# One plain chunk and two opened pairs at the start of every feed-forward block

## The chip, the cores and the metric

The kernel runs on one core of a Trainium2 chip. The metric is the device time of one execution in microseconds; lower is better. Before the change it is 2757.24 us, the median of three runs (2756.95 to 2757.96).

## What is computed

A trunk of two layers over 768 tokens (512 of one batch, 256 of another) of width 1024. Each layer is a feed-forward block, a token mixer (a gated linear recurrence in the first layer, windowed attention in the second) and a second feed-forward block. So there are four feed-forward blocks, called f0, f1, f2 and f3 here in order of time. The one that matters:

```python
def swiglu_ffn(x, w1, w2):
    gate, up = jnp.split(x @ w1, 2, axis=-1)
    return (jax.nn.silu(gate) * up) @ w2
# in each layer, twice:
x = x + 0.5 * swiglu_ffn(rmsnorm(x, g), w1, w2)
```

`w1` is 1024 x 5632 (2816 gate and 2816 up columns), `w2` is 2816 x 1024, all in float32.

## The kernel before, in words

**Precision.** Each float32 operand is split into a high part, cast by ACT, and a low part, which VectorE gets by subtracting the high part again (`split`, lines 354 to 356; for weights lines 217 and 218). A product of two operands is three matmuls: high x high, high x low, low x high (`mm3`, lines 348 to 352; `product`, lines 544 to 557). Only the low part of the weight named p5 in the first projection is subtracted by GpSimd ("POOL" in the profile), on line 218.

**Chunks and pairs.** The 2816 hidden columns are 22 chunks of 128, and the tokens are two halves of 384. A chunk that is computed plainly (`up_plain`, line 526) takes 48 matmuls of 128x384 for each token half: 8 blocks of the width, gate and up, three matmuls each. All others are done as a "pair" (`up_pair`, line 559): gate and up against the two halves of the width and the two token halves are a 2x2 matrix product, done by seven products p1 to p7 of 12 matmuls each, 84 in place of 96. p1 needs the operand `b00` and p2 needs `b10` (the two halves of the width, token half 0); p3 needs `b11` (token half 1); p7, p5, p6 and p4 need the factors t3, t1, t2 and t4, each formed by subtractions from blocks of both token halves. The weights need sums too: "third" (`a21 += a22`) and the weight s3 of p7 are made by transfers that add on landing, issued by GpSimd (`into`, line 150); "second" (`a11 += a21`) and "fourth" (`a12 += a11`) are VectorE additions on line 224, pinned to their place in the program.

**The start of a feed-forward block.** At that point the normalised input of token half 1 isn't ready yet. So the first two chunks (PLAIN = 2) are done plainly: token half 0 of both, then half 1 of both. Meanwhile three deferred steps are run from a list at six fixed places among the matmuls of half 0 (`run_later`, line 534): two that transpose token half 1 into blocks (`turn`), and `sums` (line 475), which forms the factors in eight subtractions of 128x768 and splits each (`mix`, lines 456 to 473; in f0 a step for the normalisation comes ahead of them). It does so one half of the width's blocks after the other (kp = 0, then 1), and t1, t4, t3, t2 in each.

**Order and buffers.** Instructions are recorded in the order of the code; a scheduler then sets each engine's order from what they need, but for those pinned. Each engine runs its own list strictly in order. Weights are loaded by SP's queue into four raw buffers of 512 KB (`load_next`, line 153) and are split ahead of use into eight slots `w` (`stage_next`, `ahead`). PSUM has eight banks. In the profile `wr` is a raw weight, `s` the tile of s3, `w` a split weight, `big` an operand or a factor, `tA` a hidden result, `ps` a PSUM bank, `x` the residual.

Of the kernel before, what the change touches and what calls it, by code (L numbers as in the profile page):

```python
# [16 lines left out]
P = 128  # L17
D = 1024
DFF = 2816
NC = D // P  # L20
# [34 lines left out]
class Trunk:  # L55
# [97 lines left out]
    def load_next(self):  # L153
        key, srcs, shape, how = self.queue.pop(0)
        if how in (TOK, OUT):
            self.loaded.append((len(srcs), self.tok_steps(key, srcs, how), 4))
            return
        raws = []
        for src in srcs:
            t = self.wp.tile([P, 1024], F32, tag="wr", name=self.name("wr"), bufs=RAWBUFS)  # L160
            raw = t[:, : shape[0] * shape[1]].rearrange("p (a b) -> p a b", a=shape[0])
            if len(srcs) < 4:
# [7 lines left out]
        free = 4  # L170
        if self.more.get(key):
            tail = self.tail_steps(key, self.more[key], how)
            steps = [step for both in zip(steps, tail) for step in both]
            free = 8
        self.loaded.append((len(raws), steps, free))

    def wtile(self):
        return self.wp.tile([P, 1024], F32R, tag="w", name=self.name("w"), bufs=WBUFS)
# [8 lines left out]

        return [(2, go)]

    def quad_steps(self, key, raws, srcs, order):  # L190
        nc = self.nc
        flat = lambda t: t.rearrange("p a b -> p (a b)")
        up = len(raws) == 2
        if up:
            a11, a12, a21, a22 = (flat(t[:, h : h + 4, :]) for t in raws for h in (0, 4))
            three = [srcs[1].rearrange("(k p) c -> p k c", p=P)[:, :4, :]]
        else:
            a11, a12, a21, a22 = (flat(t) for t in raws)
            three = [srcs[2][:, i : i + 1, :] for i in range(2)]
        s3 = []  # L200
        for i, src in enumerate(three):
            t = self.wp.tile([P, 512], F32, tag="s3", name=self.name("s3"), bufs=2)
            self.last_load = nc.sync.dma_start(t.rearrange("p (a b) -> p a b", a=src.shape[1]), src)
            self.into(t, a11[:, i * 512 : (i + 1) * 512])
            s3.append(t)
        self.into(a21, a22)

        def split(name, srcs, eng=None):
            if up:
                w = self.wtile()  # L210
                hi, lo = w[:, :512], w[:, 512:]
            else:
                hi, lo = self.wtile(), self.wtile()
            n = srcs[0].shape[-1]
            for i, src in enumerate(srcs):
                h, l = (t[:, i * n : (i + 1) * n] for t in (hi, lo))
                nc.scalar.copy(h, src)  # L217
                (eng or nc.vector).tensor_sub(l, src, h.bitcast(F32))  # L218
# [5 lines left out]
        add = {"second": lambda: nc.vector.tensor_add(a11, a11, a21), "fourth": lambda: nc.vector.tensor_add(a12, a12, a11)}  # L224
# [83 lines left out]
    def stage_next(self):  # L308
        if not self.loaded:
            self.load_next()  # L310
        steps = self.loaded[0][1]
        n, go = steps.pop(0)
        go()
        self.held += n
        if not steps:
            self.loaded.pop(0)
        inuse = lambda e: e[0] if len(e[1]) > e[2] or e[0] < 4 else 0
# [15 lines left out]
    def ahead(self):  # L333
        while self.queue or self.loaded:
            if not self.loaded:
                self.load_next()
            if self.held + self.loaded[0][1][0][0] > WBUFS:
                return
            self.stage_next()

# [132 lines left out]
        put("t2", b11)  # L473

    def sums(self):
        for kp in range(2):
            tiles = (self.tn[(i // 2, i % 2)][:, kp] for i in range(4))
            self.mix(*tiles, lambda name, src: self.put(name, kp, src))

    def spill_factors(self):  # L480
        self.kept = {}
# [22 lines left out]
            self.later(self.sums)  # L504

    def plan_ffn(self, tag, w1, w2):
        def up(i):
            gate, up = (w1[:, c * P : (c + 1) * P] for c in (i, NF + i))
            if i < PLAIN:
                self.plan((tag, i, 0), gate, (NC, P))  # L510
                self.plan((tag, i, 1), up, (NC, P))
            else:
                self.plan_quad((tag, i), (gate, up), (NC, P), UP)
# [12 lines left out]
    def up_plain(self, tag, j, half):  # L526
        pss = []
        for c in range(2):
            wh, wl = self.take((tag, j, c))
            ps = self.ps(H)  # L530
            for k in range(NC):
                b = self.operand(f"b{k // 4}{half}", k % 4)
                self.mm3(ps, (wh[:, k, :], wl[:, k, :]), b, k == 0, k == NC - 1)
                if half == 0 and k in (((), (2, 6)), ((3, 7), (3, 7)))[j][c]:
                    self.run_later()
            if half:
                self.done((tag, j, c))
            pss.append(ps)
        t = self.tmp(H)
        self.nc.scalar.activation(t, pss[0], AF.Silu)  # L540
        self.nc.vector.tensor_mul(t, t, pss[1])
        return t
# [16 lines left out]
    def up_pair(self, tag, j, opened=None):  # L559
# [117 lines left out]
    def ffn(self, tag, next_row):  # L677
        for g in range(GROUPS):
# [952 lines left out]
```

## Time and profile before

| | |
|---|---|
| median of three runs | 2757.24 us |
| the profiled execution, its own time | 2759.27 us |
| its span | 2757.5 us |
| granted TensorE clock | 0.999 |
| TensorE (PE) busy | 2736.1 us, 99% |
| VectorE (DVE) busy | 2201.0 us, 80% |
| ACT busy | 1396.5 us, 51% |
| GpSimd (POOL) busy | 460.7 us, 17% |

Times in the profile are microseconds from the start of the span. A timeline row is: start, duration, engine, line, operation, output <- inputs, shape and count; in brackets stands the idle time of the engine just before it and what ended that. A group's row ends with its busy time and the mean of one in ns, then the idle time of the engine ahead of them. A row with "min/median/max" has those of one instruction in ns. A row of a transfer has KB each and the median us from issue to landing. A row of the waits has the total, the number of times and the longest.

### The profile page before, as it was taken

To read this page: it belongs to the slowest core of one execution; us is meant where nothing else is said; L and a number is where in the kernel's file an instruction comes from. 1 tells how busy PE (TensorE), PEld (TensorE's weight loads), DVE (VectorE), ACT (ScalarE), POOL (GpSimd) and SP (SyncE) were. 2 spreads that over 40 slices of the span, in tenths; PEclk is the share of its full clock that TensorE was granted. 3 is DMA by queue.
4 is the path that set the end of the run, shared out by engine and by line. 5 is a ranking of instruction groups with operands and counts; after the bars stand their busy time and mean duration, and the time that the engine had idled before them with its cause. 6 is when DMAs were issued, how large, how long until landed. Compare 5 with 4: busy or idle time off the path is not lost. (4 is left out here: it accounts for less than half of the span.)

```text
span 2757.5 us, 40950 instructions
## 1 busy us (share of the span) xinstructions
PE 2736.1 (99%) x15081; PEld 2547.1 (92%) x15081; DVE 2201.0 (80%) x3766; ACT 1396.5 (51%) x2621; POOL 460.7 (17%) x507
## 2 busy tenths in 40 slices
PE   8999999999999999999999999999999999999998
PEld 8999999989999889999998999999888889999997
DVE  8788788767887888788878887887847868788877
ACT  6344444634455675444455543444458855444453
POOL 2111121200000101211120121112005611211120
PEclk9999999999999999999999999999999999999999
DMA  6554556751122743555454355545424422655453
GB/s 171 132 122 116 126 140 167 217 153 39 39 60 65 201 121 82 145 134 127 114 138 126 77 145 128 126 118 142 130 77 112 89 69 73 146 134 128 116 135 111
DMA packets 355048, 330.46 MB, mean 120 GB/s; under 512 B 14664, under 2 KB 271648, under 8 KB 354848
## 3 DMA queue, kind: packets, MB, share of 16 engines
q1 hardware_dynamic: 303744, 225.61, 27.6%
q0 software_dynamic: 46800, 88.76, 18.3%
q10 hardware_dynamic: 4304, 13.49, 1.4%
q8 instruction: 118, 1.93, 0.3%
q14 instruction: 82, 0.67, 0.1%
HBM read 226.87 MB, written 15.73 MB: 88 GB/s over the span
## 5 line engine op out<-in xcount | busy, mean ns | idle before, releaser
L549 PE MATMUL ps<-big,w 128*128 128x384 f32 x6720 | 1168.5, 334 | 0.0
L549 PEld LDWEIGHTS ps<-big,w 128*128 128x128 f32 x6720 | 1165.7, 188 | 1.4
L217 ACT CAST w<-wr 128x512 fp32r<-128x512 f32 x600 | 417.2, 706 | 651.6 <-PE ps L549 300.1
L218 DVE TENSOR_TENSOR w<-wr,w 128x512 fp32r<-128x512 f32 (+1 forms) x520 | 436.1, 842 | 138.1 <-ACT w L217 122.3
L615 PE MATMUL ps<-w,big 128*128 128x512 f32 x2016 | 460.7, 389 | 0.0
L615 PEld LDWEIGHTS ps<-w,big 128*128 128x128 f32 x2016 | 377.9, 188 | 78.8 <-DVE x L675 0.6
L151 POOL DMA_DIRECT2D s<-wr x126 | 110.5, 884 | 1220.7 <-DMA s<-in_ffn_w_dram 324.7
L675 DVE SCALAR_TENSOR_TENSOR x<-ps,x 128x512 f32<-128x512 f32 x420 | 272.7, 684 | 13.7 <-PE ps L647 13.1
L350 PE MATMUL ps<-big,w 128*128 128x384 f32 x640 | 219.2, 344 | 1.5 <-ACT w L184 1.0
L351 PE MATMUL ps<-big,w 128*128 128x384 f32 x640 | 215.1, 336 | 0.4 <-DVE big L356 0.3
L352 PE MATMUL ps<-big,w 128*128 128x384 f32 x640 | 214.5, 335 | 0.0
L355 ACT CAST big<-tA 128x384 fp32r<-128x384 f32 x308 | 153.6, 513 | 101.6 <-DVE tA L583 34.2
L356 DVE TENSOR_TENSOR big<-tA,big 128x384 fp32r<-128x384 f32 x308 | 176.3, 585 | 5.3 <-ACT big L355 3.4
L151 POOL DMA_DIRECT2D wr<-wr x109 | 95.3, 874 | 510.2 <-DMA wr<-in_ffn_w_dram 175.1
L831 PE MATMUL ps<-w,big 128*128 128x512 f32 x756 | 177.1, 392 | 0.1
L647 PE MATMUL ps<-w,big 128*128 128x512 f32 x756 | 174.5, 391 | 0.7 <-DVE x L675 0.6
L647 PEld LDWEIGHTS ps<-w,big 128*128 128x128 f32 x756 | 141.3, 188 | 30.5 <-DVE x L675 1.5
L831 PEld LDWEIGHTS ps<-w,big 128*128 128x128 f32 x756 | 140.5, 188 | 29.2 <-DVE w L356 0.6
L218 POOL TENSOR_TENSOR w<-wr,w 128x512 fp32r<-128x512 f32 x80 | 130.4, 1630 | 169.7 <-ACT w L217 152.6
L224 DVE TENSOR_TENSOR wr<-wr,wr 128x512 f32<-128x512 f32 (+1 forms) x120 | 123.6, 1030 | 20.4 <-issue 20.2
L350 PEld LDWEIGHTS ps<-big,w 128*128 128x128 f32 x640 | 120.1, 188 | 2.5 <-ACT w L184 1.3
L351 PEld LDWEIGHTS ps<-big,w 128*128 128x128 f32 x640 | 120.4, 188 | 1.4 <-DVE big L356 1.2
(219 smaller groups left out, 3647.3 us busy)
## 6 DMA issues: line engine op xcount, KB each, us to landing
wr<-in_ffn_w_dram SPq DMA_DIRECT2D x256, 512.0 KB, 4.0
s<-wr POOLq DMA_DIRECT2D x126, 256.0 KB, 4.5
s<-in_ffn_w_dram SPq DMA_DIRECT2D x120, 256.0 KB, 3.2
wr<-wr POOLq DMA_DIRECT2D x80, 256.0 KB, 3.9
wr<-in_hg_w_in_dram SPq DMA_DIRECT2D x32, 512.0 KB, 3.9
wr<-wr POOLq DMA_DIRECT2D x29, 512.0 KB, 4.6
spill<-x ACTq DMA_DIRECT2D x12, 512.0 KB, 3.9
kept<-big POOLq DMA_DIRECT2D x8, 768.0 KB, 7.9
```

The costliest lines, as they stand in the source:

```text
L151: self.nc.gpsimd.dma_start(out, src, accum_op=ALU.add)
L217: nc.scalar.copy(h, src)
L218: (eng or nc.vector).tensor_sub(l, src, h.bitcast(F32))
L350: nc.tensor.matmul(out, a[0], b[0], start=first, stop=False)
L351: nc.tensor.matmul(out, a[0], b[1], start=False, stop=False)
L352: nc.tensor.matmul(out, a[1], b[0], start=False, stop=last)
L356: self.nc.vector.tensor_sub(lo, src, hi.bitcast(F32))
L549: self.nc.tensor.matmul(ps, a[x], b[y], start=first and k == 0 and i == 0, stop=k == 3 and i == 2, skip_group_check=True,)
L615: nc.tensor.matmul(ps, a[x], w[y], start=name == chain and kp == 0 and q == 0, stop=kp == 1 and q == 2, skip_group_check=True,)
L647: nc.tensor.matmul(ps, a[x], w[y], start=name == chain and k == 0 and q == 0, stop=k == 2 and q == 2, skip_group_check=True,)
L675: self.nc.vector.scalar_tensor_tensor(x, ps, c, x, ALU.mult, ALU.add)
L831: nc.tensor.matmul(ps, x[:, sl], y, start=fresh and k == 0 and q == 0, stop=k == 3 and q == 2, skip_group_check=True,)
```

## The change

PLAIN becomes 1: only the first chunk of a block is done plainly. The next two chunks are pairs that are opened early (OPENED = 2, new function `opened_pair`): the order on PE is plain half 0, p1 of both opened pairs, p2 of both, plain half 1, then the remaining five products of the first pair and of the second. The two opened pairs are loaded as one entry that fills the four raw buffers, and their "second" and "fourth" weight sums are made by transfers (`moved=True`) and no longer by VectorE. `sums` now goes factor by factor: t3 for both kp, then t1, t2, t4. The deferred steps are run at two places in the up columns of plain half 0, behind the two p1 and behind the two p2. The 19 pairs after that and the second projection stay; which of its raw buffers an entry holds is now said by a function of the steps left. Line numbers shift: the weight split is line 228 (218 before), the transfer 153 (151), the operand split 370 (356), the subtractions of `sums` 495 (458, 459, 469 and 470), the multiply behind the plain chunk 564 (541).

GpSimd's list at the start of f1, before: the transfers for the first pair behind the plain chunks (chunk 2) and the next, p5's split of the one (line 218), transfers for the second projection's weights, p5's split of the other.

```order
L151 DMA s_1300_9150<-wr_9146 128x512
L151 DMA wr_9148<-wr_9148 128x512
L151 DMA s_1325_9262<-wr_9258 128x512
L151 DMA wr_9260<-wr_9260 128x512
L218 TENSOR_TENSOR w_9523<-wr_9148,w_9523 128x512
L151 DMA s_1392_9732<-wr_9724 128x512
L151 DMA s_1393_9735<-wr_9724 128x512
L218 TENSOR_TENSOR w_9667<-wr_9260,w_9667 128x512
```

And after: the eight transfers for both opened pairs, then p5's split of the first and of the second opened pair (line 228), then the next pair's first transfer.

```order
L153 DMA s_1305_9165<-wr_9157 128x512
L153 DMA wr_9159<-wr_9159 128x512
L153 DMA s_1306_9169<-wr_9161 128x512
L153 DMA wr_9163<-wr_9163 128x512
L153 DMA wr_9157<-wr_9159 128x512
L153 DMA wr_9161<-wr_9163 128x512
L153 DMA wr_9157<-wr_9157 128x512
L153 DMA wr_9161<-wr_9161 128x512
L228 TENSOR_TENSOR w_9428<-wr_9159,w_9428 128x512
L228 TENSOR_TENSOR w_9559<-wr_9163,w_9559 128x512
```

p5's splits of two pairs now stand next to each other behind eight transfers; the two rows of the opened pairs' "second" sums (`wr_9157<-wr_9159` and `wr_9161<-wr_9163`) and the two of their "fourth" are new there.

VectorE's list at the same place in f1, before: the end of the sums, with two weight splits and a multiply of a plain chunk among them (line 541, one input `ps` in PSUM).

```order
L356 TENSOR_TENSOR big_9399<-big_9344,big_9399 128x2x384
L356 TENSOR_TENSOR big_9402<-big_9179,big_9402 128x2x384
L459 TENSOR_TENSOR big_9305<-big_9179,big_9305 128x768
L218 TENSOR_TENSOR w_9489<-wr_9146,w_9489 128x512
L469 TENSOR_TENSOR big_9179<-big_9179,big_9344 128x768
L356 TENSOR_TENSOR big_9407<-big_9305,big_9407 128x2x384
L470 TENSOR_TENSOR big_9227<-big_9227,big_9179 128x768
L218 TENSOR_TENSOR w_9492<-s_1300_9150,w_9492 128x512
L541 TENSOR_TENSOR tA_9527<-tA_9527,ps_9495 128x384
L356 TENSOR_TENSOR big_9412<-big_9227,big_9412 128x2x384
L356 TENSOR_TENSOR big_9415<-big_9344,big_9415 128x2x384
L356 TENSOR_TENSOR big_9418<-big_9179,big_9418 128x2x384
```

After: from t2's first split to the multiply of the plain chunk's half 1 (line 564), the next step with an input in PSUM.

```order
L370 TENSOR_TENSOR big_9444<-big_9324,big_9444 128x2x384
L370 TENSOR_TENSOR big_9448<-big_9198,big_9448 128x2x384
L370 TENSOR_TENSOR big_9452<-big_9198,big_9452 128x2x384
L495 TENSOR_TENSOR big_9246<-big_9246,big_9198 128x768 x2
L228 TENSOR_TENSOR w_9476<-wr_9157,w_9476 128x512
L370 TENSOR_TENSOR big_9456<-big_9246,big_9456 128x2x384
L370 TENSOR_TENSOR big_9460<-big_9246,big_9460 128x2x384
L228 TENSOR_TENSOR w_9492<-wr_9157,w_9492 128x512
L228 TENSOR_TENSOR w_9520<-wr_9159,w_9520 128x512
L228 TENSOR_TENSOR w_9531<-s_1306_9169,w_9531 128x512
L228 TENSOR_TENSOR w_9562<-wr_9161,w_9562 128x512
L564 TENSOR_TENSOR tA_9565<-tA_9565,ps_9534 128x384
```

The multiplies that stood among the sums are gone from there but for half 0's, which stands near the start of the sums (ten rows ahead of the piece shown); the additions of line 224 are gone, and five weight splits of the opened pairs stand between the last factor and the next step from PSUM.

The diff, cut to its core:

```diff
--- before.py
+++ after.py
-PLAIN = 2
+PLAIN = 1
+OPENED = 2
...
+OPEN = ("p1", "p2", "p7", "p5", "p3", "p6", "p4")
...
+        elif how == OPEN:
+            a, b = (self.quad_steps((key[0], i + PLAIN), raws[2 * i : 2 * i + 2], srcs[2 * i : 2 * i + 2], how, True) for i in range(OPENED))
+            steps = [a[0], b[0], a[1], b[1], *a[2:], *b[2:]]
...
+        if how == OPEN:
+            inuse = lambda left: 4 if left > 5 else 2
...
+        if moved:
+            add = {"second": lambda: self.into(a11, a21), "fourth": lambda: self.into(a12, a11)}
+            behind, pin = {"p1": "second", "p2": "fourth"}, lambda ins: None
...
     def sums(self):
-        for kp in range(2):
-            tiles = (self.tn[(i // 2, i % 2)][:, kp] for i in range(4))
-            self.mix(*tiles, lambda name, src: self.put(name, kp, src))
+        sub = self.nc.vector.tensor_sub
+        b = lambda kp: [self.tn[(i // 2, i % 2)][:, kp] for i in range(4)]
+        for name, out, x, y in (("t3", 3, 1, 3), ("t1", 1, 0, 1), ("t2", 0, 0, 3), ("t4", 2, 2, 0)):
+            for kp in range(2):
+                t = b(kp)
+                sub(t[out], t[x], t[y])
+                self.put(name, kp, t[out])
 
     def spill_factors(self):
...
+            elif i == PLAIN:
+                srcs = [w for j in range(OPENED) for w in halves(i + j)]
+                self.plan_quad((tag, "open"), srcs, (NC, P), OPEN)
...
-                if half == 0 and k in (((), (2, 6)), ((3, 7), (3, 7)))[j][c]:
+                if half == 0 and c and k in (2, 6):
                     self.run_later()
...
+    def opened_pair(self, tag, j):
+        nc = self.nc
+        key = (tag, j)
+        a, v = self.ps(H), self.tmp(H)
+        p = lambda name, ps, first, last: self.product(key, name, FACTOR[name], ps, first, last)
+        p("p1", a, True, False)
+        nc.scalar.copy(v, a)
+        self.ahead()
+        yield
+        p("p2", a, False, True)
+        nc.scalar.activation(a, a, AF.Silu)
+        self.ahead()
+        yield
+        b, c, d = (self.ps(H) for _ in range(3))
+        w, t = (self.tmp(H) for _ in range(2))
+        p("p7", c, True, False)
+        nc.scalar.copy(w, c)
+        self.ahead()
+        p("p5", d, True, False)
+        nc.vector.tensor_sub(w, w, d)
+        self.ahead()
+        p("p3", d, False, True)
+        self.ahead()
+        p("p6", b, True, True)
+        nc.vector.tensor_sub(v, v, b)
+        nc.vector.tensor_add(d, v, d)
+        nc.scalar.activation(d, d, AF.Silu)
+        nc.vector.tensor_sub(w, w, v)
+        nc.vector.tensor_mul(w, w, d)
+        yield 1, w
+        self.ahead()
+        p("p4", c, False, True)
+        nc.vector.tensor_sub(t, c, v)
+        nc.vector.tensor_mul(t, t, a)
+        yield 0, t
         self.ahead()
...
+            first = {}
             if g == 0:
-                ts = {}
-                for half in range(2):
-                    for j in range(PLAIN):
-                        t = ts[2 * j + half] = self.up_plain(tag, j, half)
-                        name = f"b{j}{half}"
-                        if name != "b01":
-                            put(name, t, 0)
-                gather(ts, 0)
+                ts = {0: self.up_plain(tag, 0, 0)}
+                put("b00", ts[0], 0)
+                first = {i + PLAIN: self.opened_pair(tag, i + PLAIN) for i in range(OPENED)}
+                for _ in range(2):
+                    for pair in first.values():
+                        next(pair)
+                    self.run_later()
+                ts[1] = self.up_plain(tag, 0, 1)
                 self.run_later(len(self.deferred))
             for kp in range(2):
-                if g == 0 and kp == 0:
-                    continue
-                ts = []
+                if g or kp:
+                    ts = {}
                 for j in range(2):
-                    for half, t in enumerate(self.up_pair(tag, 4 * g + 2 * kp + j)):
-                        ts.append(t)
+                    i = 4 * g + 2 * kp + j
+                    if i < PLAIN:
+                        continue
+                    for half, t in first.get(i) or enumerate(self.up_pair(tag, i)):
+                        ts[2 * j + half] = t
                         name = f"b{j}{half}"
                         if name != "b01":
                             put(name, t, kp)
```

More of the change, by code (lines that the diff above doesn't have):

```diff
@@ L155, in load_next @@
         if how in (TOK, OUT):
-            self.loaded.append((len(srcs), self.tok_steps(key, srcs, how), 4))
+            self.loaded.append((self.tok_steps(key, srcs, how), lambda left: 4 if left > 4 else 0))
             return
@@ L167, in load_next @@
             steps = self.plain_steps(key, raws[0], shape)
+        elif how == OPEN:
+            a, b = (self.quad_steps((key[0], i + PLAIN), raws[2 * i : 2 * i + 2], srcs[2 * i : 2 * i + 2], how, True) for i in range(OPENED))
+            steps = [a[0], b[0], a[1], b[1], *a[2:], *b[2:]]
         else:
             steps = self.quad_steps(key, raws, srcs, how)
-        free = 4
-        if self.more.get(key):
-            tail = self.tail_steps(key, self.more[key], how)
+        n, more = len(raws), self.more.get(key)
+        if more:
+            tail = self.tail_steps(key, more, how)
             steps = [step for both in zip(steps, tail) for step in both]
-            free = 8
-        self.loaded.append((len(raws), steps, free))
+        if how == OPEN:
+            inuse = lambda left: 4 if left > 5 else 2
+        elif n == 4:
+            inuse = lambda left: 4 if left > (8 if more else 4) else 0
+        else:
+            inuse = lambda left: n
+        self.loaded.append((steps, inuse))
     def wtile(self):
@@ L188, in plain_steps, with quad_steps @@
         return [(2, go)]
-    def quad_steps(self, key, raws, srcs, order):
+    def quad_steps(self, key, raws, srcs, order, moved=False):
         nc = self.nc
@@ L310, in stage_next @@
             self.load_next()
-        steps = self.loaded[0][1]
+        steps = self.loaded[0][0]
         n, go = steps.pop(0)
@@ L316, in stage_next @@
             self.loaded.pop(0)
-        inuse = lambda e: e[0] if len(e[1]) > e[2] or e[0] < 4 else 0
+        inuse = lambda e: e[1](len(e[0]))
         while self.queue and sum(inuse(e) for e in self.loaded) + len(self.queue[0][1]) <= RAWBUFS:
@@ L506, in plan_ffn, with halves @@
     def plan_ffn(self, tag, w1, w2):
+        def halves(i):
+            return [w1[:, c * P : (c + 1) * P] for c in (i, NF + i)]
         def up(i):
-            gate, up = (w1[:, c * P : (c + 1) * P] for c in (i, NF + i))
             if i < PLAIN:
[L510 to L513, printed above, removed]
+                for c, w in enumerate(halves(i)):
+                    self.plan((tag, i, c), w, (NC, P))
+            elif i == PLAIN:
+                srcs = [w for j in range(OPENED) for w in halves(i + j)]
+                self.plan_quad((tag, "open"), srcs, (NC, P), OPEN)
+            elif i >= PLAIN + OPENED:
+                self.plan_quad((tag, i), halves(i), (NC, P), UP)
         for g in range(GROUPS):
@@ L591, in up_pair @@
         yield w
+        self.ahead()
[29 more added lines that the diff above has]
+        yield 1, w
+        self.ahead()
+        p("p4", c, False, True)
+        nc.vector.tensor_sub(t, c, v)
+        nc.vector.tensor_mul(t, t, a)
+        yield 0, t
         self.ahead()
```

4 lines of the change are left out of this document (2 added, 2 removed).

## The prediction, made before the changed kernel was run

> **What bounds the kernel now.** I read the page first: the busy times, the groups, the transfers.
>
> ```profile
> span 2757.5 us, 40950 instructions
> PE 2736.1 (99%) x15081; PEld 2547.1 (92%) x15081; DVE 2201.0 (80%) x3766; ACT 1396.5 (51%) x2621; POOL 460.7 (17%) x507
> L549 PE MATMUL ps<-big,w 128*128 128x384 f32 x6720 | 1168.5, 334 | 0.0
> L218 DVE TENSOR_TENSOR w<-wr,w 128x512 fp32r<-128x512 f32 (+1 forms) x520 | 436.1, 842 | 138.1 <-ACT w L217 122.3
> s<-wr POOLq DMA_DIRECT2D x126, 256.0 KB, 4.5
> wr<-wr POOLq DMA_DIRECT2D x80, 256.0 KB, 3.9
> ```
>
> TensorE is busy for 2736.1 of 2757.5 us, so the kernel is as long as its matmuls. 6720 product matmuls of 128x384 take 1168.5 us together: 0.174 us each, although one record lasts 334 ns (they overlap). The waits of PE, grouped by what ended them, confirm it; the longest stands at the very start, and the rest is small:
>
> ```profile
> PE ps L119 <- DVE stat L398: 7.6, 1, 7.6
> ```
>
> So the time changes in two ways only: fewer matmuls, or a wait in front of one that did not wait before. The change touches the first 40 us or so of each of the four FFNs (f0 to f3 in order of time), so the timeline of PE there is the next view. These rows are the first matmul of the plain chunks' token half 1 in f0, f1, f2 and f3, and in f1 the first matmul of a pair behind the plain chunks:
>
> ```profile
> 35.59 0.33 PE L350 MATMUL ps<-big,w 128*128 128x384 f32 x1
> 1043.91 0.33 PE L350 MATMUL ps<-big,w 128*128 128x384 f32 x1
> 1060.55 0.33 PE L549 MATMUL ps<-big,w 128*128 128x384 f32 x1
> 1531.39 0.33 PE L350 MATMUL ps<-big,w 128*128 128x384 f32 x1
> 2284.09 0.33 PE L350 MATMUL ps<-big,w 128*128 128x384 f32 x1
> ```
>
> Half 1 of two chunks is 96 matmuls: 1060.55 - 1043.91 = 16.64 us, 0.1733 us each, without a gap. Now VectorE beside it. First the start of its operand sums in the four FFNs, with the steps behind it in f1; then the end of the run in f1:
>
> ```profile
> 35.08 1.82 DVE L458 TENSOR_TENSOR big<-big,big 128x768 f32<-128x768 f32 x2
> ```
> ```profile
> 1038.64 0.95 DVE L458 TENSOR_TENSOR big<-big,big 128x768 f32<-128x768 f32 x1
> 1039.51 0.55 DVE L541 TENSOR_TENSOR tA<-tA,ps 128x384 f32<-128x384 f32 x1
> 1039.97 0.95 DVE L459 TENSOR_TENSOR big<-big,big 128x768 f32<-128x768 f32 x1
> ...
> 1055.64 0.55 DVE L356 TENSOR_TENSOR big<-tA,big 128x384 fp32r<-128x384 f32 x1
> 1056.11 0.69 DVE L218 TENSOR_TENSOR w<-wr,w 128x512 fp32r<-128x512 f32 x1
> ```
> ```profile
> 1527.01 1.82 DVE L458 TENSOR_TENSOR big<-big,big 128x768 f32<-128x768 f32 x2
> ```
> ```profile
> 2278.65 0.95 DVE L458 TENSOR_TENSOR big<-big,big 128x768 f32<-128x768 f32 x1
> ```
>
> A 128x768 step takes 0.87 us to the next start, a 128x384 step 0.47. From 1038.64 to 1056.11 VectorE makes 16 of the first, five of the second (three with PSUM as a source) and two 128x512 weight splits: 13.92 + 2.35 + 1.2 = 17.47 us, exactly the time between, so there is no idle time in it. VectorE is no bound over the span (80%), but it is one in these 17 us.
>
> Last, GpSimd's own vector step, the low part of p5's weight (line 218), as a group and the four at the FFN starts:
>
> ```profile
> L218 POOL TENSOR_TENSOR w<-wr,w x80: 1288/1388/8113, 45.4 to 2685.3; 128x512 fp32r<-128x512 f32 x80
> ```
> ```profile
> 45.45 8.11 POOL L218 TENSOR_TENSOR w<-wr,w 128x512 fp32r<-128x512 f32 x1 [9.17 <-ACT w L217]
> ```
> ```profile
> 1055.93 4.42 POOL L218 TENSOR_TENSOR w<-wr,w 128x512 fp32r<-128x512 f32 x1 [17.39 <-ACT w L217]
> ```
> ```profile
> 1542.73 2.76 POOL L218 TENSOR_TENSOR w<-wr,w 128x512 fp32r<-128x512 f32 x1 [17.04 <-DMA s<-in_ffn_w_dram]
> ```
> ```profile
> 2296.11 4.42 POOL L218 TENSOR_TENSOR w<-wr,w 128x512 fp32r<-128x512 f32 x1 [21.14 <-ACT w L217]
> ```
>
> The median is 1.39 us; at these four places it is 2.8 to 8.1. What ended the first two is seen on VectorE:
>
> ```profile
> 48.04 2.70 DVE L356 TENSOR_TENSOR big<-big,big 128x768 fp32r<-128x768 f32 x3
> 50.64 0.56 DVE L356 TENSOR_TENSOR big<-tA,big 128x384 fp32r<-128x384 f32 x1
> 51.11 0.70 DVE L218 TENSOR_TENSOR w<-wr,w 128x512 fp32r<-128x512 f32 x1
> 51.71 0.70 DVE L224 TENSOR_TENSOR wr<-wr,wr 128x512 f32<-128x512 f32 x1
> 52.31 0.56 DVE L541 TENSOR_TENSOR tA<-tA,ps 128x384 f32<-128x384 f32 x1
> 52.78 1.33 DVE L218 TENSOR_TENSOR w<-wr,w 128x512 fp32r<-128x512 f32 x1
> ```
> ```profile
> 1058.52 0.69 DVE L218 TENSOR_TENSOR w<-wr,w 128x512 fp32r<-128x512 f32 x1
> 1060.75 0.55 DVE L541 TENSOR_TENSOR tA<-tA,ps 128x384 f32<-128x384 f32 x1 [1.54 <-PE ps L352]
> ```
>
> In f0 GpSimd's step ends at 45.45 + 8.11 = 53.56, which is 1.25 us behind the start of a VectorE step with a PSUM source (52.31), and the VectorE step after that is stretched from 0.70 to 1.33. In f1 it ends at 1060.35, 1.2 us after VectorE falls idle near 1059.2. So while VectorE runs steps with two SBUF sources back to back, GpSimd's step stands still, and not only until the next of them ends: in f0 it let nine such ends pass.
>
> **The change part by part.** *The matmuls.* A chunk done plainly takes 96 matmuls, in a pair 84: 12 fewer in each of four FFNs, 48 x 0.174 = 8.35 us, all on PE's path. Against the profiled execution (2759.27 us, span 2757.5, 2 us above the median) as against the median of 2757.24 it is -8.35.
>
> *Sums factor by factor.* The same 16 steps of 0.87 us. In f1 p7, the first product that needs token half 1, starts after 48 plain matmuls from 1043.91: 1052.23. Its t3 is now first; both its low parts are done five steps of 0.87 and three small ones behind 1038.64, near 1044.5. The cover is the opened products and plain half 1; without it the old order's end (1055.64) would be 3.4 us late.
>
> *Sums of weights by transfers.* Four VectorE adds of 0.60 us (start to start) go per FFN and four transfers come on GpSimd's queue. Third, second and fourth sum hang on each other: 4.5 + 3.9 + 3.9 = 12.3 us. In f1 to f3 the loads run ahead under the stage before, and I cost it at nothing; without that cover a late link costs up to 3.9. In f0 there is no stage before: I put the fourth sum 2.8 us after VectorE wants it for p2's split (estimate; 0 if the loads come early, 4.5 if one transfer more is in the way), and VectorE stands for that time with the sums queued behind it. SP's loads for the next pair wait for raw buffers, which come free some 20 us ahead of need: nothing, or 4 us if that cover goes.
>
> *Deferred steps and PSUM.* The same three deferred steps, the first two in their old places; the two open accumulators leave six banks. Nothing; a late bank would cost one 0.56 us VectorE step each.
>
> *p5's split on GpSimd.* This is where I see the cost. ACT casts the opened p5's high part behind a copy that waits for p1 of the second pair, which ends at 1043.91 - 24 x 0.1733 = 1039.75. A copy and a cast such as this one
>
> ```profile
> 1048.09 0.62 ACT L217 CAST w<-wr 128x512 fp32r<-128x512 f32 x1 [1.72 <-PE ps L351]
> ```
>
> bring the split to GpSimd no earlier than 1040.9, and by 1042 with what else stands on ACT. By then VectorE has passed the one step with a PSUM source in its run (1039.51), and the next is the multiply behind plain half 1. Ahead of it stand 16 x 0.87 + 0.94 (multiply and split of half 0) + 6 weight splits x 0.60 = 18.46 us: it starts at 1038.64 + 18.46 = 1057.10, and GpSimd is done 1.25 later, at 1058.35. PE wants it in the third matmul of p5, 12 + 2 matmuls behind 1052.23: 1054.66. PE stands 3.7 us, with everything queued behind p5. The same in f3: 2278.65 + 18.46 + 1.25 = 2298.36 against 2284.09 + 62 x 0.1733 = 2294.83, 3.5 us. In f2 one weight split stands ahead of the sums and five within, the half-0 multiply is earlier: 1527.01 + 0.60 + 16.92 + 1.25 = 1545.78 against 1542.13, 3.6 us. In f0 the first p5 gets through while VectorE waits for the transfer; the second pair's is queued on GpSimd behind the next pair's third sum and meets the run: 35.08 + 16.92 + 2.8 + 1.25 = 56.05 against 35.59 + (48 + 48 + 2) x 0.1733 = 52.57, 3.5 us (0.7 to 5.2 by the bounds of the transfer). Together 14.3 us. VectorE's weight splits idle 138.1 / 520 = 0.27 us each on average; five or six per run could add 0 to 1.6 us, and as ACT is ahead in these runs I take 0.25, 1.0 in all. Stalls 15.3, matmuls -8.35: +7, **2764 us** (2766 for a profiled execution). This case's own range is 2761 to 2768.
>
> The Trainium skill, "SBUF — State Buffer", section "Who interferes with whom" (with "SBUF: two separate sides"), calls the port pair of VectorE and GpSimd an exclusive lock that whoever starts first holds for its whole instruction. That a step holds it to its end, the stretched 1.33 us agrees with; who gets it between two VectorE instructions the page does not say, and the 8.11 us show that it was not GpSimd.
>
> **The rivals.**
> *All hidden (faster).* GpSimd gets the ports at a boundary between two VectorE steps. This speaks for it:
>
> ```profile
> 1069.18 1.61 POOL L218 TENSOR_TENSOR w<-wr,w 128x512 fp32r<-128x512 f32 x1
> ```
> ```profile
> 1069.07 0.55 DVE L577 TENSOR_TENSOR tA<-tA,ps 128x384 f32<-128x384 f32 x1 [0.27 <-PE ps L549]
> 1069.78 1.58 DVE L218 TENSOR_TENSOR w<-wr,w 128x512 fp32r<-128x512 f32 x1 [0.15 <-ACT w L217]
> ```
>
> and the median of 1.39 over 80; but there VectorE had a PSUM source or a wait of its own, so the port was free. Done by 1045, p5 waits for nothing: 2757.24 - 8.35 = 2749, up to 2751 with f0's late transfer. It decides wherever the split is done within the 12 us between 1042 and 1054.66. By the skill's rule, read as first come at each boundary, GpSimd would wait 0.87 us at most, which gives this time.
>
> *Half starved.* In some FFNs VectorE waits once for an ACT cast inside the run, or its half-0 multiply slips by over 1.4 us behind 1039.51, and GpSimd slips in. Two starved of four: 7.7 - 8.35, about 2756.5. For: ACT has copies and Silus waiting for PE between its casts now. Against: f1's run has no idle time today with ACT at the same work.
>
> *Transfers late in f1 to f3 too (slower).* If the second and fourth sums land late, three more links of 3.9 us on top of starved splits give 2764 + 4 to 12, 2768 to 2776. Against: POOL is 17% busy and the loads run ahead.
>
> **How the numbers follow.** A measurement here can tell about 0.2% (5.5 us) from no change. Starved everywhere 0.55: of it 0.42 lies above 2762.8, 0.13 below. All hidden 0.27: 0.26 faster, 0.01 same. Half starved 0.13: 0.11 same, 0.02 faster. Late transfers 0.05, slower. That is faster 0.28, same 0.25, slower 0.47. The range must reach from the hidden case at 2748.5 to the starved case's end at 2768: the cases between hold most of it, and neither end can be cut with only 2 in 10 left out.
>
> **What would show it.** Right: PE waits of 3 to 4.5 us at the third matmul of the first opened p5 in f1, f2 and f3, released by GpSimd's line 228, whose record there lasts over 10 us and ends 1.25 us behind a VectorE step from PSUM; no PE wait released by a 128x768 step of the sums. Wrong: GpSimd's records there of 1.3 to 2.5 us, and PE's waits as before, with 8592 in place of 8640 matmuls of 128x384; or waits released by transfers in f1 to f3.

## The result and the profile after

The changed kernel takes 2790.59 us (median of four runs, 2789.79 to 2791.50) where the kernel before takes 2757.59 in the same comparison: a ratio of 1.012, interval 1.0102 to 1.0138. It is 33 us slower; the forecast was 2764, with a range to 2768. The page of the profiled execution, and TensorE's waits grouped by what ended them (total, times, longest):

```profile
span 2789.4 us, 41013 instructions
PE 2739.0 (98%) x15033; PEld 2546.1 (91%) x15033; DVE 2217.0 (79%) x3794; ACT 1406.6 (50%) x2649; POOL 495.1 (18%) x535
```
```profile
PE ps L572 <- DVE tA L636: 21.6, 7, 7.5
PE ps L121 <- DVE stat L412: 7.4, 1, 7.4
PE ps L572 <- POOL w L228: 3.7, 1, 3.7
PE ps L572 <- ACT tA L633: 1.5, 1, 1.5
PE ps L1510 <- ACT tA L1501: 1.3, 2, 1.1
PE ps L572 <- DVE big L370: 1.3, 1, 1.3
```

L121 and L1510 had their waits before as well (7.6 and 1.3 us, on other lines of the kernel before). New is L572, the products of the pairs. All of the loss lies in one stage. From the starts of two matmuls in each trace, the first of the plain chunk and the first of the second projection, that stage lasts:

| us | f0 | f1 | f2 | f3 |
|---|---|---|---|---|
| before | 67.0 | 65.9 | 65.3 | 65.9 |
| after | 72.4 | 74.7 | 72.7 | 76.1 |

The four differences add up to 31.9 us, all of the spans' difference (2789.4 - 2757.5). The 12 matmuls fewer per block should have made each stage 2.1 us shorter, so 40.2 us were lost. TensorE's idle time in the four stages, added up from the gaps ahead of its matmuls, grew by 28.4 us; the other 12 are matmuls at a lower clock. PE's busy time says about the same: 2739.0 in place of 2736.1 - 8.35 = 2727.8, 11.2 us more for fewer matmuls. In windows of 4 us over f3 (length, PE busy and matmuls, granted clock, DMA share, GB/s):

```profile
2330.00:2334.00 4.00, 3.42 (x20) 1.00 0.53 95
2334.00:2338.00 4.00, 0.00 (x0) 0.82 0.34 89
2338.00:2342.00 4.00, 1.06 (x3) 0.50 0.35 60
2342.00:2346.00 4.00, 4.00 (x14) 0.50 0.31 70
2346.00:2350.00 4.00, 4.00 (x23) 0.90 0.60 193
2350.00:2354.00 4.00, 4.00 (x25) 1.00 0.40 77
```

A wait of 7.5 us is followed by 14 matmuls in 4 us where 25 fit later. The Trainium skill, "TensorE: Matmul & The Clock Gate", Part 1, says that the clock falls to half after an idle window of about 3.4 us and comes back after a busy one; the 0.50 behind this wait and the return some 6 us after work resumes agree with that.

Where the longest waits come from is read backwards in f1. TensorE stood 5.88 us ahead of p3 of the second opened pair, until VectorE had read p5 out of the same PSUM bank (line 636); VectorE before that:

```profile
1084.42 0.69 PE L572 MATMUL ps<-big,w 128*128 128x384 f32 x1 [5.88 <-DVE tA L636]
```
```profile
1066.01 0.54 DVE L636 TENSOR_TENSOR tA<-tA,ps 128x384 f32<-128x384 f32 x1
...
1069.04 0.55 DVE L642 TENSOR_TENSOR ps<-tA,ps 128x384 f32<-128x384 f32 x1
1075.97 0.69 DVE L228 TENSOR_TENSOR w<-s,w 128x512 fp32r<-128x512 f32 x1 [6.38 <-ACT w L227]
...
1083.83 0.54 DVE L636 TENSOR_TENSOR tA<-tA,ps 128x384 f32<-128x384 f32 x1
```

VectorE stood 6.38 us for a weight split of the *third* pair, with the second pair's read of p5 queued behind it. ACT stood for the same weight, and behind its cast stood the second pair's copy of p7 (line 633):

```profile
1066.71 0.62 ACT L227 CAST w<-wr 128x512 fp32r<-128x512 f32 x1 [3.48 <-DMA wr<-in_ffn_w_dram]
1075.31 0.62 ACT L227 CAST w<-s 128x512 fp32r<-128x512 f32 x1 [7.97 <-DMA s<-wr]
...
1077.57 0.47 ACT L633 COPY tA<-ps 128x384 f32<-128x384 f32 x1
```

The weight is s3 of the third pair. Its transfer was issued at 1067.30 and landed 7.95 us later, where the median of before is 4.5, beside loads that SP issued at that moment:

```profile
1062.65 4.94 SPq L166 DMA_DIRECT2D wr<-in_ffn_w_dram  x4
1067.65 9.38 SPq L213 DMA_DIRECT2D s<-in_ffn_w_dram  x2
```

So the third pair's weights were asked for only at 1062.65, behind the end of plain half 1 (its last matmul starts at 1058.03), and in one burst with two more of the second projection. Before, SP issued the loads of the same pair (there the second behind the plain chunks) in f1 between 1027.11 and 1032.99, ahead of plain half 1 (from 1043.91):

```profile
1027.11 5.88 SPq L164 DMA_DIRECT2D wr<-in_ffn_w_dram  x2
```

f2 and f3 of the changed kernel show the same late load (s3 lands 6.20 and 7.53 us after its issue, waits of 5.00 and 7.52 us).

In f0 the forecast stall is there. GpSimd's split of the second p5, the VectorE step from PSUM that lets it go, and TensorE's wait:

```profile
45.48 9.97 POOL L228 TENSOR_TENSOR w<-wr,w 128x512 fp32r<-128x512 f32 x1
```
```profile
54.25 0.54 DVE L564 TENSOR_TENSOR tA<-tA,ps 128x384 f32<-128x384 f32 x1
```
```profile
55.51 0.44 PE L572 MATMUL ps<-big,w 128*128 128x384 f32 x1 [3.71 <-POOL w L228]
```

In f1 to f3 it is not. There the first p5 got through at the first end of a VectorE step in a run without gaps, and only the second was held, by then without harm; in f1:

```profile
1047.80 1.46 POOL L228 TENSOR_TENSOR w<-wr,w 128x512 fp32r<-128x512 f32 x1 [5.12 <-ACT w L227]
1060.24 5.30 POOL L228 TENSOR_TENSOR w<-wr,w 128x512 fp32r<-128x512 f32 x1 [10.97 <-ACT w L227]
```

In f2 and f3 the first took 1.92 and 1.47 us.

### The profile page after: what moved, and what is told of

It is laid out like the page before. It is cut to its first block, busy times and chain, and to the rows that moved or that the text cites. A ratio compares the mean times of both kernels' runs of the same rounds, so it can differ in the third digit from the quotient of the medians.

```text
span 2789.4 us, 41013 instructions
## 1 busy us (share of the span) xinstructions
PE 2739.0 (98%) x15033; PEld 2546.1 (91%) x15033; DVE 2217.0 (79%) x3794; ACT 1406.6 (50%) x2649; POOL 495.1 (18%) x535
## 4 chain that ended last, share of the span: by engine, by line
PE 90%; DVE 4%; ACT 3%; DMA 2%; issue 1%; POOL 0%; DVEq 0%; ACTq 0%; POOLq 0%; SPq 0%
PE ps L572 41%; PE ps L675 16%; PE ps L707 6%; PE ps L894 5%; PE ps L365 4%; PE ps L364 4%; PE ps L366 4%; PE ps L957 3%; DVE big L370 1%; PE ps L1062 1%; DVE big L495 1%; PE ps L1548 1%; DMA s<-wr 1%; ACT big L369 1%; DVE w L228 1%
## 5 line engine op out<-in xcount | busy, mean ns | idle before, releaser
L572 PE MATMUL ps<-big,w 128*128 128x384 f32 x7056 | 1240.3, 336 | 29.4 <-DVE tA L636 21.6
L572 PEld LDWEIGHTS ps<-big,w 128*128 128x128 f32 x7056 | 1231.5, 189 | 35.3 <-DVE tA L636 23.7
L227 ACT CAST w<-wr 128x512 fp32r<-128x512 f32 (+1 forms) x624 | 431.8, 703 | 648.1 <-PE ps L572 274.5
L228 DVE TENSOR_TENSOR w<-wr,w 128x512 fp32r<-128x512 f32 (+1 forms) x540 | 448.8, 835 | 134.1 <-ACT w L227 121.2
L153 POOL DMA_DIRECT2D wr<-wr x129 | 113.6, 884 | 566.2 <-DMA wr<-in_ffn_w_dram 175.5
L364 PE MATMUL ps<-big,w 128*128 128x384 f32 x512 | 176.4, 346 | 0.4 <-DVE big L443 0.2
L228 POOL TENSOR_TENSOR w<-wr,w 128x512 fp32r<-128x512 f32 x84 | 143.8, 1712 | 162.9 <-ACT w L227 162.9
L365 PE MATMUL ps<-big,w 128*128 128x384 f32 x512 | 172.3, 337 | 0.5 <-DVE big L370 0.3
L366 PE MATMUL ps<-big,w 128*128 128x384 f32 x512 | 171.5, 335 | 0.0
L228 DVE TENSOR_TENSOR w<-s,w 128x512 fp32r<-128x512 f32 x124 | 84.6, 686 | 38.0 <-ACT w L227 38.0
L600 DVE TENSOR_TENSOR tA<-tA,ps 128x384 f32<-128x384 f32 x76 | 41.8, 550 | 82.4 <-PE ps L572 82.4
```

The costliest lines, as they stand in the source:

```text
L153: self.nc.gpsimd.dma_start(out, src, accum_op=ALU.add)
L364: nc.tensor.matmul(out, a[0], b[0], start=first, stop=False)
L365: nc.tensor.matmul(out, a[0], b[1], start=False, stop=False)
L366: nc.tensor.matmul(out, a[1], b[0], start=False, stop=last)
L572: self.nc.tensor.matmul(ps, a[x], b[y], start=first and k == 0 and i == 0, stop=k == 3 and i == 2, skip_group_check=True,)
```

## The experiments

Theory A: the opened entry holds all four raw buffers, so the next loads come late and in a burst; ACT and VectorE, strictly in order, stand for them with the opened pairs' evacuations queued behind. Theory B, the prediction's: GpSimd's split is kept from the ports. Times of before in these comparisons are 2757.8 to 2758.4.

**pin_next_pair.** The third pair's splits are queued behind the second opened pair's copy of p7 and read of p5.

```diff
-        go()
+        with ExitStack() as behind:
+            for ins in self.pins if steps is not self.open_steps else ():
+                behind.enter_context(self.tc.issue_after(ins))
+            go()
...
+        if last:
+            self.pins = [copied, read]
```

> Edit: in the changed kernel the weight splits of the third pair (the first one behind the two opened pairs) are queued on ACT and on VectorE behind the second opened pair's copy of p7 and its read of p5 from PSUM. Nothing is left out. Theory A (in-order queues behind a late load): in f1 to f3 TensorE's long waits at the second opened pair's p3 (5.88, 5.00 and 7.52 us, ended by VectorE's read of p5) go, and with them the stretch at about half clock behind each; the sum is 2790.6 - 18.4 - some 9 = about 2763, up to 2768 if p7 of the third pair then waits a little for its weight. Theory B (the prediction's: GpSimd's p5 split kept from the SBUF ports): those waits stay, 2789 to 2792.

2783.68 us (1.0093, 1.0064 to 1.0122). The waits at p3 that the read of p5 ends fell from 21.6 us to 2.6, as A has it, but the time did not follow: the stage of f1 shrank from 74.7 to 66.7 us and that of f3 from 76.1 to 67.4, but what follows them grew by 4.5 and 6.6 us. The late weights now stop something else: ACT's copies of the third pair (4.7 us in all) and the second projection's first additions, as in f3:

```profile
2355.34 0.47 PE L688 MATMUL ps<-w,big 128*128 128x512 f32 x1 [3.70 <-DVE x L748]
```

So the queue says who waits, and the late weights that somebody waits.

**no_s3_transfer.** The third pair's p7 takes another raw weight.

```diff
+            if key[1] == PLAIN + OPENED:
+                three = []
...
+        s3 = s3 or [a12]
```

> Edit: the third pair's s3 is neither loaded nor made by a transfer; its p7 takes another raw weight in its place, so this leaves out part of the computation. Theory A: ACT's wait of 6 to 8 us for that transfer goes in f1 to f3, the long waits at p3 with it, but the wait for the load itself (3.5 to 5.6 us on ACT) stays: about 2763 to 2772. Theory B: no change, 2789 to 2792. A rival of A, that the load and not the transfer is what is late: the waits at p3 stay above 3 us each, 2775 to 2785.

2771.89 us (1.0055, 1.0035 to 1.0074): one load and one transfer of 256 KB per block, left out, give back 18.7 of the 33 us. The waits that are left:

```profile
PE ps L575 <- DVE tA L639: 7.5, 7, 2.6
PE ps L121 <- DMA tB<-in_hg_g_norm_dram: 7.3, 1, 7.3
PE ps L575 <- POOL w L231: 3.7, 1, 3.7
```

**two_buffers.** The second opened pair's weights are not loaded; its splits read the first's raw weight.

```diff
-        for src in srcs:
+        for src in srcs[:2] if how == OPEN else srcs:
...
-            inuse = lambda left: 4 if left > 5 else 2
+            inuse = lambda left: 2
```

> Edit: the second opened pair's weights are not loaded; its products take splits of the first's raw weight, so this leaves out two loads and the second pair's sums per block (other results, the same matmuls and splits). The opened entry holds two raw buffers and not four, so the third pair can be loaded at once; nothing else about it changes. Theory A, in full (the four raw buffers held through plain half 1 make every following load late): the long waits of f1 to f3 go and the first stage of the second projection does not wait either, 2762 to 2771, what stays being f0 and waits of about 1 us at p3. If the transfer is slow for another reason: 2785 or more.

2774.10 us (1.0058, 1.0038 to 1.0078), 3 us above the range. With the buffers free the stage of f2 lasts 65.1 us (72.7) and that of f3 68.0 (76.1). The edit also takes away two loads and the second pair's weight sums, so that fewer transfers may be part of this. f1 stayed slow, for theory B's reason. GpSimd's split of the first p5, and TensorE behind it:

```profile
1048.11 16.61 POOL L230 TENSOR_TENSOR w<-wr,w 128x512 fp32r<-128x512 f32 x1 [8.46 <-ACT w L229]
```
```profile
1064.77 0.69 PE L576 MATMUL ps<-big,w 128*128 128x384 f32 x1 [3.69 <-POOL w L230]
```

This is the stall that the prediction put into f1, and its price: VectorE's next step from PSUM starts at 1063.51, GpSimd ends 1.21 us later, TensorE waited 3.69 us. In f3 the first p5 was held too, without this price:

```profile
2294.93 13.36 POOL L230 TENSOR_TENSOR w<-wr,w 128x512 fp32r<-128x512 f32 x1 [10.55 <-ACT w L229]
```
```profile
2306.18 2.92 DVE L374 TENSOR_TENSOR big<-big,big 128x768 fp32r<-128x768 f32 x2
```

It ended at 2308.29, between two VectorE steps with both inputs in SBUF, the second of which is stretched (two such steps take 1.82 us elsewhere in the run). No step from PSUM was needed, and no matmul waited for it (a weight load did, for 0.4 us).

**p5_on_vector.**

```diff
-            split(name, own[name], nc.gpsimd if up and name == "p5" else None)
+            split(name, own[name], nc.gpsimd if up and name == "p5" and not moved else None)
```

> Edit: the opened pairs' p5 low parts are subtracted by VectorE in place of GpSimd. Theory B: all of the extra waits hang on GpSimd's held split, so f0's 3.71 us and the waits in f1 to f3 go: below 2765. Theory A: only f0's 3.71 us goes and the slower clock behind it, some 5 us in all, and two more steps of 0.60 us stand in VectorE's run: 2784 to 2788, with the long waits of f1 to f3 as they were.

2783.44 us (1.0092, 1.0063 to 1.0121), at the lower end of A's range. GpSimd's wait in f0 is gone, the three long ones stay (4.82, 5.02 and 4.71 us, those of f1 and f3 shorter than they were): A and not B. In f0 the third pair's third weight sum took its place (ACT stood 6.65 us for it): the stage lasts 72.9 us as against 72.4.

```profile
PE ps L572 <- DVE tA L636: 15.8, 4, 5.0
PE ps L121 <- DMA tB<-in_hg_g_norm_dram: 7.6, 1, 7.6
PE ps L572 <- ACT tA L633: 2.9, 1, 2.9
```

**sums_by_vector.**

```diff
         if moved:
-            add = {"second": lambda: self.into(a11, a21), "fourth": lambda: self.into(a12, a11)}
```

> Edit: the opened pairs' second and fourth weight sums are made by VectorE additions again, at the same places, in place of the eight transfers. Theory C (these transfers are what is late): f0's waits of 0.55, 1.29 and 3.71 us shrink, and the long ones in f1 to f3 too, below 2775. Theory A: four more steps of 0.60 us stand in VectorE's gap-free run per block, the raw buffers come free 2.4 us later, and each long wait grows by about that: 2795 to 2802.

2790.73 us (1.0118, 1.0089 to 1.0148): the same time as with the transfers, so neither theory's number. The edit takes back four of the opened pairs' eight transfers, the second and fourth sums; these four are not the cause, and the other four (s3 and the third sums) stayed; the waits only moved (3.35 us for a VectorE split at 36 us in f0, 3.70 us for GpSimd's p5 at 1067 in f1).

**vec_s3.** The third pair's s3 and third sum by VectorE.

```diff
+        late = up and key[1] == PLAIN + OPENED
...
-            self.into(t, a11[:, i * 512 : (i + 1) * 512])
+            if late:
+                nc.vector.tensor_add(t, t, a11)
+            else:
+                self.into(t, a11[:, i * 512 : (i + 1) * 512])
...
-        self.into(a21, a22)
+        if late:
+            nc.vector.tensor_add(a21, a21, a22)
+        else:
+            self.into(a21, a22)
```

> Edit: the third pair's s3 and its third weight sum are made by one VectorE addition each in place of a transfer. All the work is done. Theory A (a transfer of 7 to 8 us behind a late load, with VectorE and ACT queued behind it): as with the s3 left out (2771.9) or a little below, since the other late transfer goes too: 2765 to 2773; what stays is f0. If the load alone were late: above 2780.

2776.23 us (1.0069, 1.0046 to 1.0092), 3 us above the range of A. f1 to f3 last 67.3, 69.2 and 66.7 us; f0 keeps its GpSimd wait (4.30 us here), and the second projection begins to wait (5.6 us).

**vec_s3_p5.** The last two edits together.

> Edit: the former one, and the opened pairs' p5 low parts on VectorE. Theory A + B (late transfer in f1 to f3 and f0, held GpSimd split in f0 and, in part, f1 to f3): both causes gone, 2751 to 2760. Theory D (VectorE's run itself is the bound behind plain half 1, with now four more steps of 0.60 us in it per block): waits of 1 to 3 us at the second and third products of the opened pairs in each block, 2762 to 2772.

2769.04 us (1.0039, 1.0020 to 1.0059). The number is D's and not A's; the place is neither's. In the opened pairs no wait is over 1.1 us now, and the stages last 68.7, 65.8, 64.1 and 65.6 us, together as long as before; the 11.5 us by which the span is longer than before have come up behind them, with waits of 1.3 to 2.9 us in the second projection.

**p3_last.**

```diff
-OPEN = ("p1", "p2", "p7", "p5", "p3", "p6", "p4")
+OPEN = ("p1", "p2", "p7", "p5", "p6", "p4", "p3")
...
-        p("p3", d, False, True)
-        self.ahead()
         p("p6", b, True, True)
...
         p("p4", c, False, True)
...
+        p("p3", d, False, True)
```

> Edit: in the opened pairs p3 comes last (p7, p5, p6, p4, p3) as in the ordinary pairs, so that 24 matmuls (4.2 us) lie between p5 and the product that needs VectorE's read of p5. Theory A: each long wait shrinks by about 4 us, 2770 to 2780 with the faster clock. Theory E (the order of the products is the whole cause): the waits at p3 go, below 2765. If the order does not matter: 2788 to 2792.

2791.36 us (1.0122, 1.0089 to 1.0155): a miss. The waits on the read of p5 fell to 4.1 us, but ACT's copy (7.4 us) and the second projection (4.9 us) took over, and half clock followed these as well. The order of the products is not the cause.

**vec_s3_p5_p3.** All three edits.

> Edit: all three: the third pair's two sums and the opened p5 splits on VectorE, and p3 last. Theory A + B: 2749 to 2756, faster than before by up to 8 us. Theory D: what is left are waits on VectorE's run at t1 or t4, 2756 to 2768.

2766.25 us (1.0032, 1.0020 to 1.0044): again D's number, at another place than D's. The stages are now shorter than before by 0.5, 1.3, 1.3 and 0.9 us, yet the kernel isn't: TensorE waits in the second projection.

```profile
PE ps L682 <- DVE x L742: 8.7, 5, 2.7
```
```profile
1089.33 2.00 ACT L234 CAST w<-wr 128x1024 fp32r<-128x1024 f32 x2 [7.47 <-PE ps L579]
```
```profile
1084.01 0.88 POOL L153 DMA_DIRECT2D wr<-wr  x1 [13.27 <-DVE tA L607]
```

That cast of a second projection's weight also waits for its third sum, a transfer issued at 1084.01 that landed at 1089.17, just ahead of it: PE, named as the releaser, was not the last. It is the same effect one entry on, since this entry's raw buffers come free late too.

**vec_all.** That sum by VectorE as well.

```diff
-        if late:
+        if late or key[1:] == ("down", 0):
             nc.vector.tensor_add(a21, a21, a22)
```

> Edit: as the last of the former (third pair's sums and opened p5 splits on VectorE, p3 last), and the third weight sum of the first stage of the second projection by one VectorE addition in place of a transfer, since in the former run ACT stood 7.5 us for that transfer and the 5.7 us lost in f1 came there. Theory A: these waits of 1.4 to 2.8 us at the head of that stage go, 2752 to 2758, at best 5 us faster than before. Theory D (VectorE's backlog): they stay, 2762 to 2768.

2755.76 us (ten runs, 2754.66 to 2756.54) as against 2757.92 (13 runs, 2757.26 to 2758.74): a ratio of 0.9992, interval 0.9983 to 1.0002. No run of the one reaches into the other's, but the interval touches 1: it undoes all of the loss, and a gain of about 2 us is likely and not settled.

```profile
span 2753.9 us, 40991 instructions
...
PE 2729.6 (99%) x15033; PEld 2538.2 (92%) x15033; DVE 2220.5 (81%) x3814; ACT 1406.6 (51%) x2649; POOL 452.0 (16%) x515
```
```profile
PE ps L579 <- DVE tA L643: 1.9, 4, 0.7
```

PE's busy time is 6.5 us below that of before, near the 8.35 of the 48 matmuls, and the clock stays full.

**vec_all_p5_back.** The former with the opened p5 splits on GpSimd again.

> Edit: the fastest version so far (2755.8), with the opened pairs' p5 low parts on GpSimd again, so that this one thing differs. Theory B with its price: in f0 the second p5's split is held until VectorE's multiply from PSUM, a wait of 3.5 to 4.3 us and some 2 us of slower clock; in f1 to f3 a wait of 3.7 us wherever GpSimd loses the ports at p5 of the first pair (it lost them in one of six blocks seen so far), otherwise none: 2761 to 2764, up to 2776 if it loses everywhere. If the split costs nothing once the late loads are gone: 2754 to 2757.

2766.49 us (ten runs, 2761.30 to 2769.55; 1.0025, 1.0016 to 1.0035), above the 2761 to 2764 expected: by the medians the split on GpSimd costs 10.7 us by itself, and its runs lie 8 us apart where those of vec_all lie 2 apart. In the profiled one it lost the ports in f1 (one row for both splits) and won in f0:

```profile
1041.95 18.29 POOL L235 TENSOR_TENSOR w<-wr,w 128x512 fp32r<-128x512 f32 x2 [5.06 <-ACT w L234]
```
```profile
1058.61 0.69 PE L579 MATMUL ps<-big,w 128*128 128x384 f32 x1 [3.67 <-POOL w L235]
```

The Trainium skill, "SBUF — State Buffer", section "SBUF: two separate sides", lets the one of the two engines that starts first have the ports for its whole instruction. These rows add that at the end of a VectorE step in a gap-free run either may be next: GpSimd was, within 2 us, in f1, f2 and f3 of the changed kernel, and was not for some 16 us in f1 here and in two_buffers. In f3 here it was held for 13.36 us, as in two_buffers; no matmul waited for it, but TensorE stood 3.4 us for ACT and VectorE later in that stage. So of the six blocks of the changed kernel and two_buffers that the expectation counts, the ports were lost in two and not in one, and a lost block has no fixed price.

**old_sums.** The changed kernel with the old order of the operand sums.

```diff
-        for name, out, x, y in (("t3", 3, 1, 3), ("t1", 1, 0, 1), ("t2", 0, 0, 3), ("t4", 2, 2, 0)):
-            for kp in range(2):
...
+        for kp in range(2):
+            tiles = (self.tn[(i // 2, i % 2)][:, kp] for i in range(4))
+            self.mix(*tiles, lambda name, src: self.put(name, kp, src))
```

> Edit: the changed kernel with the old order of the operand sums (kp by kp, t1, t4, t3, t2). Theory A: t3 of kp 1 is then ready some 8 us after plain half 1 ends, so TensorE waits for a VectorE split (line 370) ahead of p7 in each block, but the late load is covered by that wait in part: 2792 to 2810. If the new order were itself a cost: below 2788.

2776.78 us (1.0068, 1.0048 to 1.0088): 14 us faster than the changed kernel where 2 to 20 slower was expected (two runs, 6 us apart); it is the expectation's other case, a cost of the new order. The wait for t3 is there (3.88 us in f0, 0.85 to 1.75 after). But the third pair's loads start earlier and apart from the next ones:

```profile
1062.23 4.73 SPq L166 DMA_DIRECT2D wr<-in_ffn_w_dram  x2
```

with plain half 1's last matmul at 1062.82, so 0.6 us ahead of it and not 4.6 us behind, and the longest wait in f1 to f3 is 2.61 us, not 7.52. In the new order the opened pairs' splits come later among the sums and free their raw buffers later. That this is the whole of the 14 us was not tested apart.

## Why the prediction was wrong

*The bound, the matmuls.* Right: TensorE sets the time, and in vec_all, without the stalls, its busy time falls by 6.5 of the 8.35 us.

*Sums factor by factor.* Their own cost was right (no long wait for t3). What the order does to the weight splits behind it was not seen, and it is part of the loss (old_sums).

*Sums of weights by transfers.* Costed at nothing in f1 to f3; with the second and fourth sums on VectorE the time is the same (sums_by_vector), so the exchange costs nothing on balance. In f0 VectorE stood 1.09 us for the split of a transferred sum, where 2.8 was put.

*SP's loads.* This is the step that failed: "SP's loads for the next pair wait for raw buffers, which come free some 20 us ahead of need: nothing, or 4 us if that cover goes." Need was taken as the moment when TensorE reaches the third pair. But ACT and VectorE meet its splits some 13 us earlier (from 1066 on in f1, when without stalls TensorE would come to the pair 21 us behind plain half 1, near 1079), since the list puts them among the opened pairs' evacuations; there the cover was gone. The price was not 4 us either, but 5.0 to 7.5 us of wait in each of f1 to f3. These stages lost 26.5 us together against before; with no_s3_transfer, two_buffers and vec_s3 5.3, 8.0 and 6.1 us of that are left, though a part comes back in the second projection. The first two leave work out; vec_s3 does all of it. The rival with late transfers came nearest, with a chance of 0.05 and 2768 to 2776; but it named the opened pairs' second and fourth sums, and the late ones were the third pair's weights.

*The PSUM bank.* "Nothing" for PSUM overlooked that p3 goes into the bank that p5 was in, and must wait for VectorE's read of p5. It is where the wait shows, not why it is there (p3_last, pin_next_pair).

*p5's split on GpSimd.* This term, 14.3 us, was mis-sized: it came to 3.71 us. The price was right in f0 (3.5 us forecast) and in f1 where it happened (3.7 forecast, 3.69 and 3.67 in two_buffers and vec_all_p5_back); the count was not. It happened in one of four blocks of the changed kernel and not in four, because whether GpSimd gets the ports at a boundary is not fixed; the forecast took it as lost until the next step from PSUM everywhere, and in f3 of two_buffers and vec_all_p5_back it came in earlier, at no wait. That the kernel would be slower was forecast, but mostly for this reason, which made up 3.7 of the 28 us of added waits: the direction was in the main luck.

*The clock.* Not in the sum at all: the 40 us lost are 28 us of waits and, by subtraction, 12 of half clock behind them.

## What to carry to other kernels

Ask of each load when its first reader comes up in the in-order list of ACT or VectorE, not when TensorE needs the result, and what else is queued behind that reader; an entry that holds every staging buffer moves all loads after it into one burst. When taking away one late step, look at the next entry in the same queue: here the stall turned up in a new place with each step until the last. Add to a TensorE wait of several microseconds about half as much again for the slow clock after it (12 us behind 28 here).

## What the runs showed of the hardware that was not expected

GpSimd can lose the SBUF ports to VectorE for 16.6 us in a row, get them in the midst of a gap-free run after 13.36 us, or get them at the first boundary, in the same place of the same kernel's blocks; a version that hangs on it varies by 8 us between runs. Half clock followed each of the waits of 3.7 us and more in these stages. Behind shorter ones it came in some cases, as after one of 1.87 us (pin_next_pair, 1102 to 1108 us, clock 0.5), and not in others, as after one of 2.92 us (p5_on_vector, 66.8 us). Transfers that add on landing took 5.8 to 8.6 us in f1 to f3 of the changed kernel beside four loads of 512 KB, as against 3.3 once those had landed. That the loads alone slow them is not shown: in f1 of old_sums, with the loads issued further apart, the same two transfers took 6.4 and 7.2 us.
